# Splitting the downward weights of an FFN anew in every block instead of storing the parts

## The chip, the cores and the metric

The kernel runs on one core of a Trainium2 chip. The metric is the device time of one execution in microseconds, the median of several runs. TensorE (PE) multiplies, VectorE (DVE) and ScalarE (ACT) work elementwise, GpSimd (POOL) does small steps, and SyncE (SP) issues every DMA.

## The reference

One layer of a streaming encoder on 2048 new frames (a prompt) and on 32 frames of a running stream (a sample), width 1024, all in float32:

```
proj = rmsnorm(x) @ w_in                       # q, k, v, u, gate
o    = stick-breaking attention(q, k, v)       # 8 heads of 64
c    = silu(layernorm(dwconv31(u * sigmoid(gate))))
h    = x + concat([o, c]) @ w_out
up   = rmsnorm(h) @ w_up                       # 1024 -> 2 * 2816
a, g = split(dwconv3(up))
y    = h + (silu(g) * a) @ w_down              # 2816 -> 1024
```

The outputs are y of both streams, the new keys and values, and the states of the two convolutions. The change concerns the last line alone.

## The kernel before

**Split products.** Matmuls run on a float32r type. To keep float32 accuracy each operand is split into a high part (rounded to float32r) and a low part (the rest), and a product is the sum of three: high x high, low x high, high x low. The splitting is done by this helper:

```
def split(hi, lo, src):
    act(hi, src, AF.Copy)                                       # ScalarE
    vec.tensor_tensor(lo, src, hi.bitcast(F32), ALU.subtract)   # VectorE
```

**Stages.** A first phase makes q, k, v, u and gate for the whole prompt. Then the FFN runs in four blocks of 512 rows, `feed(0)` to `feed(3)`; the last block also takes the 32 rows of the sample. While blocks 0 to 2 run, other work is woven in: in block 0 the attention of the sample and part of the convolution, in block 1 the attention of rows 1024 and up, in block 2 its last part and the convolution of the last block; and in each of them `project` makes h of the next block. Block 3 has nothing woven in.

**Inside a block.** The 2816 channels are 22 tiles of 128 (f = 0 to 21; FT is 22). `up(f)` loads the up weights of two tiles (the linear and the gated half) in two parts each, multiplies, copies the sums out of PSUM (ScalarE), runs the 3-tap convolution (VectorE), applies silu and the product, and splits the result into `ah` and `al`. At its end it brings in wd, the downward weights of tile f: 128 rows of 1024, high and low. Tiles are taken in pairs (GRP is 2): `down` multiplies a pair after `up` of the first tile of the next pair, and VectorE adds the PSUM sums to y in SBUF. For the last pairs the order shifts by one: the pair 18, 19 is multiplied after `up(21)`, and the pair 20, 21 after that.

**Buffers.** SBUF is laid out by hand in two arenas, `arena` (float32) and `arena_r` (float32r). A name has a fixed list of places that are used in turn, by the order in which the program asks:

```
"raw": spots(8192, 512, 3),      # in arena: three pieces of 128x512
"jk": [9216],                    # the same words as the third raw
"wu": spots(24576, 2048, 2),     # in arena_r
"wd": spots(28672, 2048, 3),
"wdx": [26624],                  # the second wu
```

wd has three places, and the last tile of a block takes `wdx`. The raw pieces of w_up (block 0) and of w_out (`project`, by `out_weights`, which puts its parts into wu) go through the three places of `raw`. `norm_rows`, which norms h for the next block after `up(19)`, writes its squares to `jk`.

**Weights in DRAM.** In block 0 the raw weights are loaded, split, and both parts are stored to scratch tensors `wu_d` and `wd_d` in DRAM. Blocks 1 to 3 load the parts from there, 1 MB for each tile.

**Order.** The program is written as steps for a planner (`Plan`). It knows what every step reads and writes, gives each a price and a rank (the order in the program, or later if a step that it needs is later), simulates the five engines, and fixes an order of instructions for each engine, SP's DMA issues too. An engine takes the ready step of lowest rank. The DMA issues are one queue: an issue that waits (for a buffer to come free, say) holds up those behind it.

Of the kernel before, what the change touches and what calls it, by code (L numbers as in the profile page):

```python
# [11 lines left out]
F32R = mybir.dt.float32r  # L12
# [7 lines left out]
P = 128  # L20
# [12 lines left out]
FT = FF // P  # L33
# [338 lines left out]
def hybrid_step_kernel(  # L372
# [97 lines left out]
    def run(ap):  # L470

        n = 1
        for step, size in reversed(ap.ap):
            if step != n:
                break
            n *= size
        return n

    def dma(dst, src, gets=(), puts=()):
        dst, src = (x.bitcast(F32) if x.dtype == F32R else x for x in (dst, src))  # L480
        ns = dst.size() * 4 / 360 * (1 if min(run(dst), run(src)) >= 128 else 2)
        plan.add("sp", ns, lambda: nc.sync.dma_start(dst, src), [dst], [src], gets, puts)  # L482
# [9 lines left out]
    dram = ctx.enter_context(tc.tile_pool(name="dram", bufs=1, space=DRAM))  # L492
# [11 lines left out]
    c_d = dram.tile([SB, CB], F32, name="c_d")[:]  # L504

    wu_d = dram.tile([2 * FT, P, 2048], F32R, name="wu_d")[:]
    wd_d = dram.tile([FT, P, 2048], F32R, name="wd_d")[:]

    cst = ctx.enter_context(tc.tile_pool(name="cst", bufs=1))

# [42 lines left out]
    def slot(tag, shape, dtype=F32):  # L553
        at = SLOTS[tag]
        i = turns[tag] = (turns.get(tag, -1) + 1) % len(at)
        return place(at[i], shape, dtype)
# [22 lines left out]
    def split(hi, lo, src):  # L579
        act(hi, src, AF.Copy)  # L580
        vec.tensor_tensor(lo, src, hi.bitcast(F32), ALU.subtract)
# [631 lines left out]
    def feed(b, upto):  # L1213
# [5 lines left out]
        n = n_p + n_s  # L1219
# [18 lines left out]
        def up(f):  # L1238
            accs = []
            for part in range(2):  # L1240
                fi = part * FT + f
                wu = slot("wu", (2, KT, P), F32R)
                if b == 0:
                    for j in range(2):
                        raw = slot("raw", (4, P))
# [51 lines left out]
            ah, al = slot("ah" + tag, (w,), F32R), slot("al" + tag, (w,), F32R)  # L1297
            split(ah, al, aa)
            wd = slot("wdx" if f == FT - 1 else "wd", (2, D), F32R)
            if b == 0:  # L1300
                for j in range(2):
                    cs = slice(j * 512, (j + 1) * 512)
                    raw = slot("raw", (512,))
                    dma(raw, w_down[f * P : (f + 1) * P, cs])
                    split(wd[:, 0, cs], wd[:, 1, cs], raw)
                dma(wd_d[f], wd.rearrange("p a n -> p (a n)"), puts=[("wd", f)])
            else:
                dma(wd.rearrange("p a n -> p (a n)"), wd_d[f], gets=[("wd", f)])
            return ah, al, wd

        sums = slot("yc", (KT, PS + 2)) if n_s else None
# [185 lines left out]
```

## Time and profile before

| what | us |
|---|---|
| time, median of 3 runs | 2927.1 (2920.81 to 2928.97) |
| the profiled execution, its own time | 2924.49 |
| its span, from the first to the last instruction | 2922.7 |
| TensorE busy | 2729.2 |
| VectorE busy | 2041.6 |
| ScalarE busy | 1147.4 |

The profile is of one execution. Busy times of engines overlap, so they don't add up to the span. A time on its own in a row of a timeline or of the chain is counted from the start of the span.

### The profile page before, as it was taken

What the parts mean: (1) busy time and instruction counts of PE and PEld (TensorE: products, weight loads), DVE (VectorE), ACT (ScalarE), POOL (GpSimd) and SP (SyncE); (2) the same over time, 40 slices, a digit from 0 to 9 for tenths busy, and PEclk for the clock granted to TensorE, in tenths of its full rate; (3) what the DMA queues carried; (4) which work ended last, traced back from release to release, by engine and by line L of the source; (5) the groups of instructions that cost most, each with busy time, mean ns of one, the idle gap of its engine ahead of it and who ended that gap; (6) DMA issues with size and microseconds to landing.
All of it is one profiled execution on the core that took longest, in us unless ns stands there. A gap on an engine that the chain in (4) does not pass through costs nothing.

```text
span 2922.7 us, 42946 instructions
## 1 busy us (share of the span) xinstructions
PE 2729.2 (93%) x16218; PEld 2391.3 (82%) x16218; DVE 2041.6 (70%) x3055; ACT 1147.4 (39%) x2087; POOL 395.1 (14%) x809
## 2 busy tenths in 40 slices
PE   7998999989889999999999999999999979999999
PEld 7988898888767777778888877887777857899998
DVE  3476578679799776658887776779889745444444
ACT  4144434345544444435454454344444423211111
POOL 1144113224111010100000010001011000000000
PEclk9999999999899999999999999999999989999999
DMA  5255546654687998874555547664554466544443
GB/s 168 77 167 161 152 142 190 202 176 130 185 282 260 304 304 263 288 260 163 184 180 177 185 164 219 245 214 156 171 171 158 148 216 215 208 173 173 173 173 133
DMA packets 290696, 563.44 MB, mean 193 GB/s; under 512 B 33810, under 2 KB 175518, under 8 KB 256697
## 3 DMA queue, kind: packets, MB, share of 16 engines
q1 hardware_dynamic: 290489, 560.71, 58.4%
q8 instruction: 127, 2.08, 0.3%
q14 instruction: 80, 0.66, 0.1%
HBM read 410.14 MB, written 146.22 MB: 190 GB/s over the span
## 4 chain that ended last, share of the span: by engine, by line
PE 47%; DVE 13%; DMA 10%; ACT 4%; issue 4%; POOL 2%; SPq 1%; POOLq 0%; DVEq 0%; ACTq 0%
PE bank L424 44%; DVE arena L453 10%; DMA arena_r<-wu_d 4%; PE bank L431 3%; DVE arena_r L453 3%; ACT arena L438 2%; DMA arena<-in_w_up_dram 2%; ACT arena_r L438 1%; SPq L482 1%; ACT L438 1%; DMA h_d<-arena 1%; POOL arena L453 1%; POOL few L453 1%; DMA arena<-oT_d 1%; DMA arena<-in_w_out_dram 0%
## 5 line engine op out<-in xcount | busy, mean ns | idle before, releaser
L424 PE MATMUL bank<-arena_r 128*128 128x512 f32 (+6 forms) x14224 | 2544.8, 338 | 90.0 <-DMA arena_r<-wu_d 26.1
L424 PEld LDWEIGHTS bank<-arena_r 128*128 128x128 f32 x14224 | 2180.4, 192 | 378.8 <-DVE arena_r L453 33.1
L438 ACT ACTIVATE arena<-bank 128x512 f32<-128x512 f32 (+8 forms) x699 | 333.4, 501 | 859.4 <-PE bank L424 654.6
L438 ACT ACTIVATE arena_r<-arena 128x512 fp32r<-128x512 f32 (+2 forms) x428 | 288.4, 682 | 430.0 <-DVE arena L453 95.2
L453 DVE TENSOR_TENSOR arena<-bank,arena 128x512 f32<-128x512 f32 (+3 forms) x488 | 305.8, 635 | 182.5 <-PE bank L424 155.4
L453 DVE TENSOR_TENSOR_SCAN arena<-arena 128x512 f32<-128x512 f32 (+4 forms) x332 | 365.1, 1106 | 66.8 <-ACT arena L438 38.9
L453 DVE SCALAR_TENSOR_TENSOR arena<-arena,wdw 128x512 f32<-128x512 f32 (+1 forms) x600 | 402.0, 670 | 8.0
L453 DVE TENSOR_TENSOR arena_r<-arena,arena_r 128x512 fp32r<-128x512 f32 (+2 forms) x428 | 321.6, 765 | 105.8 <-ACT arena_r L438 103.5
L438 ACT ACTIVATE arena_r<-bank 128x512 fp32r<-128x512 f32 (+1 forms) x388 | 202.4, 562 | 283.0 <-PE bank L431 268.4
L431 PE MATMUL bank<-ident,arena 128*128 128x128 f32 (+5 forms) x1654 | 235.8, 279 | 74.1 <-DVE arena L453 59.6
L453 DVE TENSOR_SCALAR arena<-arena,wfd,bfd 128x512 f32<-128x512 f32 (+1 forms) x176 | 97.5, 554 | 293.6 <-ACT arena L438 293.6
L431 PEld LDWEIGHTS bank<-ident,arena 128*128 128x128 f32 (+5 forms) x1654 | 190.6, 143 | 114.9 <-DVE arena L453 77.8
L453 DVE SCALAR_TENSOR_TENSOR arena<-arena,wfd 128x512 f32<-128x512 f32 (+1 forms) x352 | 265.6, 755 | 8.7 <-DVE arena L453 0.5
L453 POOL COPY halo<-arena 128x2 f32<-128x2 f32 x220 | 55.6, 266 | 1293.0 <-ACT arena L438 1262.5
L453 DVE TENSOR_TENSOR arena_r<-bank,arena_r 128x512 fp32r<-128x512 f32 (+3 forms) x300 | 184.1, 640 | 56.7 <-ACT arena_r L438 55.9
L438 ACT ACT_TABLE_LOAD x107 | 137.3, 1283 | 8.5 <-DVE arena L453 5.5
L438 ACT ACTIVATE arena<-arena 128x512 f32<-128x512 f32 (+3 forms) x122 | 92.1, 756 | 110.3 <-DVE arena L453 97.3
L453 POOL TENSOR_SCALAR_AFFINE_SELECT arena<-arena 128x128 f32<-128x128 f32 x128 | 60.1, 476 | 426.5 <-ACT arena L438 423.7
L453 DVE TENSOR_TENSOR arena<-arena 128x512 f32<-128x512 f32 (+3 forms) x97 | 71.4, 736 | 61.8 <-ACT arena L438 35.0
L453 POOL TENSOR_TENSOR few<-few,nhalf 128x1 f32<-128x1 f32 (+3 forms) x87 | 101.3, 1164 | 7.1
L453 POOL TENSOR_SCALAR few<-few 128x1 f32<-128x1 f32 (+3 forms) x87 | 38.0, 437 | 446.4 <-DVE few L453 307.3
L453 POOL COPY arena<-halo 128x2 f32<-128x2 f32 x176 | 68.7, 391 | 184.6 <-DVE arena L453 177.9
(48 smaller groups left out, 449.9 us busy)
## 6 DMA issues: line engine op xcount, KB each, us to landing
arena_r<-wu_d SPq DMA_DIRECT2D x132, 1024.0 KB
arena_r<-wd_d SPq DMA_DIRECT2D x66, 1024.0 KB
wu_d<-arena_r SPq DMA_DIRECT2D x44, 1024.0 KB
arena<-in_w_up_dram SPq DMA_DIRECT2D x88, 256.0 KB
wd_d<-arena_r SPq DMA_DIRECT2D x22, 1024.0 KB
arena_r<-kT_d SPq DMA_DIRECT2D x80, 256.0 KB
arena_r<-dv_d SPq DMA_DIRECT2D x80, 256.0 KB
arena<-in_w_out_dram SPq DMA_DIRECT2D x80, 256.0 KB
```

The costliest lines, as they stand in the source:

```text
L424: lambda: nc.tensor.matmul(plan.real(out), lhsT, rhs, start=start, stop=stop),
L431: "pe", in_.shape[0] * (0.4167 if in_.dtype == F32R else 0.8333) + 2.5, lambda: nc.tensor.transpose(plan.real(out), in_, idt), [out], [in_ ...
L438: "act", ns, lambda: nc.scalar.activation(out, plan.real(in_), func, **kw), aps(out, kw.get("accum_out")), reads
L453: self.tag, self.price(name, n / (2 if fast else 1), pointers), lambda: fn(out, *map(plan.real, args), **kw), [out], aps(*args, *kw.values())
L482: plan.add("sp", ns, lambda: nc.sync.dma_start(dst, src), [dst], [src], gets, puts)
```

## The change

In every block, block 0 or not, each tile's downward weights are loaded raw in two pieces of 128x512 (256 KB) and split. The parts are no longer stored, and the scratch tensor `wd_d` is gone. The up weights are treated as before.

```diff
     wu_d = dram.tile([2 * FT, P, 2048], F32R, name="wu_d")[:]
-    wd_d = dram.tile([FT, P, 2048], F32R, name="wd_d")[:]
...
             wd = slot("wdx" if f == FT - 1 else "wd", (2, D), F32R)
-            if b == 0:
-                for j in range(2):
-                    cs = slice(j * 512, (j + 1) * 512)
-                    raw = slot("raw", (512,))
-                    dma(raw, w_down[f * P : (f + 1) * P, cs])
-                    split(wd[:, 0, cs], wd[:, 1, cs], raw)
-                dma(wd_d[f], wd.rearrange("p a n -> p (a n)"), puts=[("wd", f)])
-            else:
-                dma(wd.rearrange("p a n -> p (a n)"), wd_d[f], gets=[("wd", f)])
+            for j in range(2):
+                cs = slice(j * 512, (j + 1) * 512)
+                raw = slot("raw", (512,))
+                dma(raw, w_down[f * P : (f + 1) * P, cs])
+                split(wd[:, 0, cs], wd[:, 1, cs], raw)
             return ah, al, wd
```

## Rows read from the trace of the kernel before

**Rows 1.** The page: busy us, share of the span, instructions of each engine.

```profile
PE 2729.2 (93%) x16218; PEld 2391.3 (82%) x16218; DVE 2041.6 (70%) x3055; ACT 1147.4 (39%) x2087; POOL 395.1 (14%) x809
```

**Rows 2.** Busy times by stretch; its first row names the columns.

```profile
core 0: us, PE busy (x) PEld busy (x) DVE busy (x) ACT busy (x) POOL busy (x), PEclk, DMA share, GB/s
760.00:860.00 100.00, 81.27 (x376) 65.18 (x375) 84.11 (x132) 49.83 (x92) 16.86 (x32) 0.86 0.73 237
...
760.00:1260.00 500.00, 461.10 (x2113) 370.45 (x2113) 379.48 (x590) 236.28 (x392) 62.30 (x135) 0.96 0.84 275
1260.00:1835.00 575.00, 551.34 (x2862) 462.56 (x2861) 432.12 (x596) 259.58 (x437) 44.00 (x124) 0.99 0.57 190
1835.00:2330.00 495.00, 468.83 (x2400) 391.26 (x2399) 423.12 (x689) 214.40 (x354) 49.65 (x115) 0.99 0.52 180
2330.00:2412.00 82.00, 66.07 (x284) 50.09 (x283) 42.47 (x63) 22.32 (x39) 4.38 (x11) 0.90 0.68 214
2412.00:2923.00 511.00, 488.25 (x3309) 456.00 (x3307) 244.34 (x389) 100.09 (x247) 38.19 (x197) 0.99 0.50 179
2000.00:2240.00 240.00, 222.29 (x1146) 185.36 (x1145) 221.83 (x358) 98.71 (x166) 24.97 (x46) 0.99 0.48 163
```

**Rows 3.** Waits, 760 to 1260: engine, line, waited for, us, times, longest.

```profile
PE bank L424 <- ACT arena_r L438: 13.7, 6, 6.5
PE bank L424 <- DVE arena_r L453: 8.9, 10, 2.4
...
ACT arena_r L438 <- DMA arena<-in_w_up_dram: 60.9, 41, 4.5
```

**Rows 4.** Waits of TensorE, 1260 to 1835.

```profile
PE bank L431 <- DVE arena L453: 15.7, 14, 4.9
PE bank L424 <- DVE arena_r L453: 3.4, 3, 2.2
```

**Rows 5.** Waits of TensorE, 1835 to 2330.

```profile
PE bank L431 <- DVE arena L453: 12.8, 15, 1.6
PE bank L424 <- ACT arena L438: 6.2, 4, 2.2
PE bank L431 <- ACT arena L438: 3.8, 3, 1.5
```

**Rows 6.** Waits of TensorE, 2412 to the end.

```profile
PE bank L424 <- DMA arena_r<-wu_d: 14.4, 14, 2.4
```

**Rows 7.** The chain that ended last, by line: 1260 to 1835, then 1835 to 2330.

```profile
by line: PE bank L424 63.2%; DVE arena L453 7.9%; PE bank L431 7.3%; issue 6.4%; DMA arena_r<-wu_d 4.6%; ACT arena L438 3.1%; ACT L438 2.4%; DMA h_d<-arena 1.7%; DMA arena_r<-kT_d 1.4%; DVE arena_r L453 0.9%; DMA arena<-oT_d 0.8%; POOL aren
by line: PE bank L424 48.8%; DVE arena L453 26.4%; PE bank L431 6.1%; issue 4.0%; DVE arena_r L453 3.8%; ACT L438 3.4%; DMA arena_r<-wu_d 3.0%; ACT arena L438 2.8%; ACT arena_r L438 1.3%; POOL arena L453 0.3%; POOL halo L453 0.2%; ACTq L438
```

**Rows 8.** Groups by shape, 1260 to 1835: busy us, mean ns, idle before.

```profile
L453 DVE TENSOR_TENSOR arena_r<-arena,arena_r 128x512 fp32r<-128x512 f32 x39 | 26.3, 682 | 7.2 <-ACT arena_r L438 7.2
L438 ACT ACTIVATE arena_r<-arena 128x512 fp32r<-128x512 f32 x39 | 24.4, 629 | 17.3 <-DVE arena L453 10.6 <-PE bank L424 5.2 <-issue 1.2
```

**Rows 9.** Timeline of VectorE at 2442: start us, us, instruction.

```profile
2442.69 1.89 DVE L453 TENSOR_TENSOR arena_r<-arena,arena_r 128x512 fp32r<-128x512 f32 x3
```

**Rows 10.** Timeline of TensorE at the end of block 0: [idle before <- releaser].

```profile
1227.18 1.95 PE L424 MATMUL bank<-arena_r 128*128 128x512 f32 x3 [6.53 <-ACT arena_r L438]
```

**Rows 11.** Timeline of SP before block 3: issues of DMAs.

```profile
2383.49 0.84 SPq L482 DMA_DIRECT2D arena_r<-wd_d  x2
```

**Rows 12.** Pieces of the chain: start us, us from issue to landing.

```profile
769.63 3.62 DMA arena<-in_w_up_dram
...
2385.84 7.98 DMA arena<-in_w_out_dram
...
2599.80 6.62 DMA arena_r<-wu_d
...
2672.99 7.57 DMA arena_r<-wu_d
...
2877.88 6.40 DMA arena_r<-wu_d
```

## The prediction

> **What bounds the kernel now.** I read the page first. TensorE is busy for 2729.2 of 2922.7 us, VectorE for 2041.6 [rows 1]: what the change can win or lose is what TensorE waits, some 7% of the span, and not the sum of what it moves. The change touches only the four passes of the FFN, so I cut the span there: block 0 (760 to 1260 us), block 1 (to 1835), block 2 (to 2330), the hand-over to block 3 (to 2412), block 3 (to the end). The busy times of these stretches [rows 2] give TensorE's idle time: 39 us of 500, 24 of 575, 26 of 495, 16 of 82 and 23 of 511. Reading on in the same rows, the second engine differs by stage. In block 0 it is the DMA engines (share 0.84, 275 GB/s). In block 2 it is VectorE: 423.12 of 495 us, and 221.83 of 240 us from 2000 to 2240. In block 3 nothing else is near full (VectorE 244 of 511 us, DMA share 0.50).
>
> Then I asked what TensorE waits for in each stretch. In block 0 it is splits: 13.7 us on ScalarE's half, 8.9 us on VectorE's [rows 3], and ScalarE itself waits 60.9 us for raw up weights to land. In block 1 it waits for VectorE's scans (15.7 us) and differences (3.4 us) [rows 4]. In block 2 it waits for VectorE (12.8 us) and for ScalarE's copies and sigmoids (6.2 and 3.8 us) [rows 5]. In block 3 it is the landing of the up weights, 14.4 us in 14 waits [rows 6]. The chain of waits says the same: VectorE holds 26.4 + 3.8 = 30% of it in block 2 and 7.9 + 0.9 = 9% in block 1 [rows 7]. No row has TensorE waiting for the downward weights.
>
> **The change, part by part.** *Removed:* 22 stores of 1 MB, one for each f of block 0, and 66 loads of 1 MB in blocks 1 to 3. *Added:* in each of blocks 1 to 3, 44 raw loads of 256 KB, 44 copies on ScalarE and 44 subtractions on VectorE. Half the bytes are loaded, and the work goes to the two engines that TensorE already waits for.
>
> The same split of a 128x512 piece is in block 1 already: 629 ns for the copy, 682 ns for the difference [rows 8]. Instructions of VectorE overlap at their ends: three differences in a row took 1.89 us [rows 9], so one more costs (1.89 - 0.68) / 2 = 0.60 us of the engine. That is 44 x 0.60 = 26.4 us of VectorE and at most 44 x 0.63 = 27.7 us of ScalarE in a block of 500 to 575 us. ScalarE is busy for 260 of 575 us in block 1 and less elsewhere [rows 2], so its time is covered. Behind a copy that waits for its raw piece, or for the wd buffer that TensorE still reads, stand ScalarE's PSUM copies, for which VectorE and then TensorE wait. The planner puts the copy where it models the buffer as free, so I take nothing for that and leave it to the range.
>
> *Block 0.* Its bytes fall by 22 x 1.05 = 23 MB of 500 us x 275 GB/s = 137 MB, so the DMA share falls from 0.84 to about 0.70, and SP no longer holds a store back until VectorE has written the low half. What can come back is TensorE's wait for splits that wait for raw weights: of the 13.7 us [rows 3] one wait of 6.53 us is at the hand-over [rows 10], where ScalarE was busy with the norms of the next block; 7.2 us are left. Bounds 0 (the up weights keep their own chain of raw buffer, split and store) and -13.7. I take about half of the 7.2, -4 us, because most of the weights still moved are up weights.
>
> *Block 1.* Two readings. By the chain, VectorE sets 9% of the stretch: 0.088 x 26.4 = 2.3 us. By idle time: VectorE's goes from 575 - 432 = 143 us to 117, and if the 19.1 us that TensorE waits for it [rows 4] grow in that ratio (1.22), +4.2 us. I take +3; bounds 0 (the planner fits the splits into gaps) and +9, twice the second reading.
>
> *Block 2 to 2330.* Some 38 of the 44 splits lie here (495 of the 575 us or so between two hand-overs): 38 x 0.60 = 22.8 us on an engine with 72 us idle. By the chain: 0.302 x 22.8 = 6.9 us. By idle time: 72 / 49 = 1.47, and 22.8 us of waits for VectorE and ScalarE [rows 5] grow by 10.7 us. I take the chain's figure, +7, since the weight copies of this block may be put later, where VectorE is free; bounds 0 and +22.8, each split on the path.
>
> *Hand-over from block 2 to 3.* At 2383.49 two loads of 1 MB of wd are issued [rows 11], and the w_out piece behind them in the chain, issued at 2385.84, takes 7.98 us to land; a raw piece of the same 256 KB took 3.62 us at 769.63, the shortest that I found [rows 12]. ScalarE's copy of it, and TensorE behind that, can only come after. With a quarter of the bytes in each load ahead of it, at best 7.98 - 3.62 = 4.4 us come back; I take half, -2. On the other side the w_down pieces now pass through the same three raw buffers as the w_out pieces, and the third of them is also the scratch of the norms' squares (jk): up to +8.6 us, priced with the second rival.
>
> The Trainium skill speaks against this gain. Its page "DMA: Bandwidth & Descriptors" (Rules for kernel authors) asks for 1 MiB or more in one DMA, and its section "Anatomy of one DMA" fits a transfer as about 2.0 us plus the bytes at 436 GB/s, though for GpSimd's path: two pieces of 256 KB would be an estimated 5.2 us where one of 1 MB is 4.4, so halving the bytes would save no landing time. By that the hand-over gives 0 and not -2, block 3 too gains nothing, and the sum is +6. The rows agree that a small piece is dear (3.62 us for 256 KB against 6.40 us for 1 MB of wu), but not that two in flight cost twice that, which no row here shows.
>
> *Block 3.* Here TensorE waits for wu, and each load of it is issued when its buffer comes free. The waits are mostly at the first load after a pair's product, 4.4 us behind two wd loads of 1 MB: in the chain that load takes 6.62 to 7.57 us in five pairs (mean 7.03), and 6.40 us at 2877.88, with no wd near [rows 12]. Over 11 pairs 0.63 us each is 6.9 us. The raw pieces carry half the bytes, and they wait for a raw buffer and not for the wd buffer, so many will land earlier: I take -3, bounds -6.9 and 0. VectorE has half its time free here, so its 26.4 us cost nothing; without that cover they would be all of the cost. The last f's wd goes into a buffer (wdx) that up still reads; its raw pieces can land before that ends, and four short instructions then stand where a whole load stood.
>
> The sum is -4 + 3 + 7 - 2 - 3 = +1 us. The profiled execution took 2924.49 us (span 2922.7), so 2925.5 on its scale; the median of the three timed runs lies 2.6 us higher, at 2927.1, and on that scale I forecast **2928 us**. About 0.3% (8.8 us) is what a measurement can tell from no change; the three runs themselves spread over 8 us.
>
> **The rivals.** *First, VectorE becomes the bound of block 2 (slower).* Place: 2000 to 2240, where it is busy for 92% [rows 2]. Price: all 22.8 us there and the 4.2 us of block 1, less the 4 of block 0 and the 3 of block 3: +20, 2947 us. It decides when the convolution, scans and differences of that stretch can't move past 2240. For it: 30% of the chain. Against it: VectorE needs only 42 of 82 us from 2330 on, and the planner knows its price for each split.
>
> *Second, the raw buffers become the wait at the hand-overs (slower).* The downward pieces of f = 20 and 21 come behind the norms' squares in the third raw buffer, and these wait for the last rows of h. In block 0, where it is so already, TensorE lost 6.53 us at 1227 [rows 10]; I add a third for the splits that come late behind it: 8.6 us. At both later hand-overs that is +17 on top of +1: 2945 us (one alone 2937). It decides when the pieces land after TensorE has ended the product of f = 18 and 19. Against it: these products alone are 48 matmuls of 128x512, and the weights that they need are not held up.
>
> *Third, the freed DMA time is the larger part (faster).* Block 0 gives back all 13.7 us, the hand-over 4.4, block 3 6.9, and the splits find gaps in blocks 1 and 2 for all but 2 us: -23, 2904 us. For it: ScalarE's 60.9 us of waiting for raw up weights [rows 3], and the wu that lands late behind wd. Against it: TensorE is idle for 39 us in the whole block 0, and 18.7 us of that lies in its first 100 us [rows 2], where the FFN only starts.
>
> **How the numbers follow.** Chances: the forecast 0.43, first rival 0.20, second 0.14, third 0.23. The range is 2906 to 2948 us: it takes in the first two rivals and nearly reaches the third, whose time needs all its parts at their bounds. What it leaves out is mishaps added together above and such a full gain below. The forecast's own range is 2918 to 2938. Faster: 0.21 from the third rival and 0.03 from the forecast's lower edge, 0.24. Slower: 0.18 and 0.12 from the first two and 0.03 from the forecast's upper edge, 0.33. Within 0.3%: the rest, 0.43.
>
> **What would show it.** Block 0's DMA share near 0.70 and TensorE's waits for splits there some 4 us shorter; 83 copies and 83 differences of 128x512 (39 + 44) in block 1, and VectorE at 458 of 575 us; in block 2 a larger share of VectorE in the chain and 7 us more; in block 3 some 3 us less of waits for wu. The prediction is wrong if the planner, given other steps, orders a hand-over quite differently: one gap there is worth more than any of my terms. It is also wrong if ScalarE's copies wait for TensorE's buffers with the PSUM copies stuck behind them, which would show as waits of TensorE for ScalarE in block 3.

## The result, and the profile after

The changed kernel took 2908.03 us (median of 4 runs, 2898.65 to 2910.15) where the kernel before took 2926.45 on the same chip. The ratio is 0.9945, with a 95% interval of 0.9927 to 0.9962: 18 us less. A second comparison gave 2912.56 against 2919.88, ratio 0.9970 (0.9958 to 0.9982): 7 us less. Both are faster by more than the error. Their intervals just overlap; their mean is 13 us. The forecast, 1 us more than before (2928 us), lies 20 us above the time of the first comparison and some 14 us above the mean of the two.

The profiled execution of the changed kernel took 2898.65 us (span 2896.8). It is the fastest of the four by 9 us, so its profile shows the kernel at its best. Its busy times, to be set beside [rows 1]:

```profile
PE 2723.3 (94%) x16218; PEld 2387.5 (82%) x16218; DVE 2109.2 (73%) x3187; ACT 1221.9 (42%) x2217; POOL 402.4 (14%) x809
```

VectorE has 132 more instructions, as the change says (3 blocks of 44 splits), and 67.6 us more work. ScalarE has 74.5 us more: 132 more copies and two table loads fewer. TensorE's busy time is 6 us less and its idle time 20 us less (193.5 us before, 173.5 after). Its stretches, to be set beside [rows 2], with the same columns:

```profile
760.00:1260.00 500.00, 463.90 (x2118) 375.67 (x2118) 381.98 (x600) 238.77 (x393) 56.60 (x135) 0.96 0.74 232
1260.00:1835.00 575.00, 556.58 (x2908) 466.57 (x2908) 453.04 (x635) 286.64 (x487) 50.11 (x131) 1.00 0.55 177
1835.00:2330.00 495.00, 467.94 (x2386) 388.38 (x2385) 446.43 (x734) 235.12 (x391) 60.76 (x114) 0.99 0.47 154
2330.00:2412.00 82.00, 72.39 (x306) 55.54 (x305) 43.50 (x66) 21.33 (x37) 2.67 (x10) 0.94 0.67 207
2412.00:2897.00 485.00, 468.11 (x3230) 440.34 (x3228) 264.11 (x425) 124.20 (x288) 36.56 (x192) 0.99 0.46 157
2000.00:2240.00 240.00, 221.49 (x1120) 182.60 (x1119) 224.79 (x374) 110.16 (x182) 36.24 (x49) 0.98 0.46 149
```

VectorE's share rises in every stretch, and TensorE's falls in none by more than half a point. But these windows are fixed in time, so they hold different work in the two kernels once a gain has shifted it. The rest therefore goes by marks in the work: VectorE's first convolution step of each tile, read from its timeline. The time between two marks is the length of a stretch, whatever came before it. Single executions scatter by a few us in each stretch (the two profiles of the changed kernel have spans of 2896.8 and 2916.2 us), so the table takes the mean over all kernels profiled for this study that have the old path in a stretch, and over all that have the new one there (the kernel without the difference, below, is in none; a kernel that has the old path on one side of a hand-over and the new one on the other is left out of it; of block 3 only the plain old and new paths count, and the one with more places for wd). It is worked out from those timelines:

```
stretch (block, tiles)  old path there: n, mean (range)   new path there: n, mean (range)  difference
block 0, 0 to end       13  483.8 (481.4 to 487.2)         4  483.2 (480.1 to 487.4)   -0.6
block 1, 0 to 4          7   82.7 (80.9 to 86.1)          10   78.0 (77.4 to 78.8)     -4.7
block 1, 4 to 18        10  369.8 (368.0 to 371.4)         7  370.0 (368.0 to 371.3)   +0.2
hand-over 1 to 2        10  158.5 (156.3 to 160.9)         7  158.0 (153.1 to 160.1)   -0.6
block 2, 0 to 18        10  453.6 (452.0 to 455.5)         7  456.9 (455.1 to 457.7)   +3.3
hand-over 2 to 3         6  158.1 (155.9 to 159.6)         7  157.5 (155.7 to 160.5)   -0.6
block 3, 0 to 20         5  361.9 (360.1 to 363.5)         6  355.2 (354.6 to 356.1)   -6.7
```

A hand-over is from tile 18 of one block to tile 0 of the next. For block 0 the new path means that no stores of the downward parts stand in the plan. The differences add up to -9.7 us, between the two timed ones (-7 and -18). Two rows carry it, the first tiles of block 1 and block 3: in both the ranges of the two columns do not touch.

Two more numbers are used below. They are worked out from the same traces for the same stretches. One is TensorE's idle time. The other is what its clock costs: the trace records when the granted clock was 0.5, the lower of its two levels (1.2 GHz), and half of that time is counted as lost. In block 3 TensorE's idle time falls by 5.1 us and the clock's cost stays. In the first tiles of block 1 the idle time falls by 2.7 us and the clock's cost by 1.2. In block 2 the idle time grows by 1.2 us and the clock's cost by 1.4.

### The profile page after: what moved, and what is told of

Read it like the earlier page. It is cut to its first block, busy times and chain, and to the rows that moved or that the text cites. A ratio compares the mean times of both kernels' runs of the same rounds, so it can differ in the third digit from the quotient of the medians.

```text
span 2896.8 us, 43450 instructions
## 1 busy us (share of the span) xinstructions
PE 2723.3 (94%) x16218; PEld 2387.5 (82%) x16218; DVE 2109.2 (73%) x3187; ACT 1221.9 (42%) x2217; POOL 402.4 (14%) x809
## 4 chain that ended last, share of the span: by engine, by line
PE 45%; DVE 15%; DMA 9%; issue 5%; ACT 5%; SPq 1%; POOL 1%; POOLq 0%; ACTq 0%; DVEq 0%
PE bank L424 42%; DVE arena L453 11%; DVE arena_r L453 4%; PE bank L431 3%; ACT arena L438 2%; DMA arena_r<-wu_d 2%; DMA arena<-in_w_up_dram 2%; ACT arena_r L438 1%; ACT L438 1%; SPq L482 1%; DMA arena<-in_w_down_dram 1%; DMA arena<-in_w_out_dram 1%; POOL arena L453 1%; DMA arena_r<-qT_d 1%; DMA h_d<-arena 1%
## 5 line engine op out<-in xcount | busy, mean ns | idle before, releaser
L438 ACT ACTIVATE arena_r<-arena 128x512 fp32r<-128x512 f32 (+3 forms) x560 | 370.4, 671 | 552.6 <-PE bank L424 173.3
L453 DVE TENSOR_TENSOR arena_r<-arena,arena_r 128x512 fp32r<-128x512 f32 (+3 forms) x560 | 407.2, 739 | 149.9 <-ACT arena_r L438 147.0
L453 POOL COPY halo<-arena 128x2 f32<-128x2 f32 x220 | 62.0, 295 | 1246.0 <-ACT arena L438 1218.3
```

The source lines that it names most:

```text
L438: "act", ns, lambda: nc.scalar.activation(out, plan.real(in_), func, **kw), aps(out, kw.get("accum_out")), reads
L453: self.tag, self.price(name, n / (2 if fast else 1), pointers), lambda: fn(out, *map(plan.real, args), **kw), [out], aps(*args, *kw.values())
```

## The experiments

The theories: that the gain comes from the stores of block 0 (S in the expectations), from the halved bytes of the loads, or from their earlier issue; and that VectorE pays for it in blocks 1 and 2. Ratios are against the kernel before, run on the same chip, with 95% intervals.

**The stores of block 0.** My first reading of the two traces was that the gain came from block 0: TensorE's wait of 6.53 us at its end [rows 10] is gone in the changed kernel. Three kernels take it apart. The first keeps the stores in the changed kernel:

```diff
                 split(wd[:, 0, cs], wd[:, 1, cs], raw)
+            if b == 0:
+                dma(wd_d[f], wd.rearrange("p a n -> p (a n)"), puts=[("wd", f)])
```

> The changed kernel, with the 22 stores of both parts to a scratch tensor in block 0 kept, though nothing reads them; nothing else is undone. Theory S (the stores of block 0 were the cost: they fill the DMA queue and hold wd and raw buffers there): the early gain goes, about 10 us of it (in the profile after, the first step of the third tile of block 1 comes 11.7 us earlier than before, 1.2 of it from ahead of block 0), so some 2918 us. Theory R (the loads of blocks 1 to 3 are the cost: a load of both parts waits for the wd buffer that TensorE reads, and then lands beside the loads of up weights): within 3 us of the changed kernel, 2908. Theory P (the planner's new order at the hand-overs, by luck, is the gain): the order changes again, and the time may be anything between 2905 and 2930, the change showing at a hand-over and not inside a block.

Measured: 0.9973 (0.9961 to 0.9986). Still faster than before, with all the stores.

The second takes the stores out of the kernel before; blocks 1 to 3 load 1 MB from the scratch tensor of the up weights:

```diff
...
-                dma(wd_d[f], wd.rearrange("p a n -> p (a n)"), puts=[("wd", f)])
             else:
-                dma(wd.rearrange("p a n -> p (a n)"), wd_d[f], gets=[("wd", f)])
+                dma(wd.rearrange("p a n -> p (a n)"), wu_d[f], gets=[("wu", f)])
```

> The kernel before, without the stores of block 0; in blocks 1 to 3 wd is loaded in one piece of 1 MB as before, from the scratch tensor of the up weights, so y of these blocks is computed with other weights. Theory S: the gain of block 0 and its hand-over alone, about 10 us, so 2916; blocks 1 to 3 as before, with some 11 us of waits of TensorE for up weights in block 3. Theory R: no gain, 2926. Theory P: anything.

Measured: 0.9995 (0.9979 to 1.0011). Without the stores alone no gain is to be seen. The third has the first one's order, but each store moves 64 KB on the chip while the planner reckons with 1 MB (its edit against the first one, in short):

```diff
-                dma(wd_d[f], wd.rearrange("p a n -> p (a n)"), puts=[("wd", f)])
+                part = wd.rearrange("p a n -> p (a n)")[:, :128].bitcast(F32)
+                plan.add("sp", P * 2048 * 4 / 360, lambda: nc.sync.dma_start(wd_d[f][:, :128].bitcast(F32), part), ...)
```

> The changed kernel with the 22 stores of block 0 as steps of the planner, priced as 1 MB each, but of 64 KB on the chip: the order is that of the kernel with the stores kept, the traffic that of the changed one. Theory S by traffic (the stores held up the raw up weights in the DMA queue): the 6.5 us wait of TensorE for a split at the end of block 0 goes, and its time comes to that of the changed kernel, about 2908. Theory S by the order (the planner, with stores in its queue, puts the norms of the next block ahead of that split on ScalarE): the wait of 6.5 us stays, and the time is that of the kernel with the stores kept, 0.997 of before.

Measured: 0.9946 (0.9934 to 0.9958). TensorE's waits from 1180 to 1260 us, first of the changed kernel, then of this one:

```profile
PE bank L424 <- ACT arena_r L438: 3.3, 1, 3.3
```

```profile
PE bank L424 <- ACT arena_r L438: 6.9, 2, 6.5
```

The long wait comes back though the traffic stays away. So it belongs to the planned order, not to the bytes. It is also worth nothing on balance: without stores in the plan the tiles from 18 to 20 are 9 us shorter (37 us against 46 to 47), but tiles 8 to 16 are some 8 us longer (184 to 188 us against 175 to 179) and the way from 20 to block 1 another 3. The theory that the stores set the gain falls. This kernel was timed below the one that really stores (0.9946 against 0.9973, in two comparisons on two chips). The traces of the two hold the same instructions of VectorE, ScalarE, GpSimd and SyncE in the same order. Their profiles differ by 1.0 us in block 0, where the stores are, and by 9.0 us from there to tile 20 of block 3, where nothing is stored for wd. So a cost of the traffic does not show where it would have to arise, and what made the two comparisons differ is open.

**Block 3 alone.** The kernel before, with the new path in block 3 only:

```diff
-            if b == 0:
+            if b == 0 or last_b:
...
-                dma(wd_d[f], wd.rearrange("p a n -> p (a n)"), puts=[("wd", f)])
+                if b == 0:
+                    dma(wd_d[f], wd.rearrange("p a n -> p (a n)"), puts=[("wd", f)])
```

> The kernel before, but block 3 loads its downward weights raw and splits them; blocks 0 to 2 as before, with the stores. Theory R: block 3 is 6 to 9 us shorter (in the profiles, 25.9 less 16.9), all of it in waits of TensorE for up weights, 10.8 us to some 5; so about 2918. Theory S: no gain. Theory P: no gain in block 3, since nothing is woven in there and its order of matmuls is fixed.

Measured: 0.9994 (0.9982 to 1.0006), though its block 3 took 356.1 us like the changed kernel's. The hand-over ahead of it took 162.2 us, longer than in any kernel with the old path throughout (155.9 to 159.6): much of the gain was taken back there. More on that below.

Is it the earlier issue, or the fewer bytes? One kernel gives wd seven places in block 3, so that its loads need not wait for TensorE:

```diff
+    "wd3": spots(28672, 2048, 3, 0, 2048, 4096, 6144),
...
-            wd = slot("wdx" if f == FT - 1 else "wd", (2, D), F32R)
+            wd = slot("wd3" if last_b else "wdx" if f == FT - 1 else "wd", (2, D), F32R)
```

> The kernel before, but in block 3 wd has seven buffers and not three and one (four of them where the normed rows of blocks 0 to 2 lay), so that the loads of both parts can be issued several tiles ahead. The bytes and the engines' work are those of before. Theory R, by the wait for the buffer: the same 6 to 9 us in block 3 as from the raw loads, 2918. Theory B (it is the halved bytes in block 3): no gain, 2926, waits for up weights near 11 us.

Measured: 1.0009 (0.9996 to 1.0023), block 3 in 363.5 us. It is inconclusive on its own: the loads were free to go, but they still went out in pairs, 4.4 us ahead of the wu load. The next one adds the bytes back to the kernel with block 3 alone, as a second load of each raw piece to a place that nobody reads:

```diff
+    "dum": spots(9728, 512, 6),
...
+                    if last_b:
+                        dma(slot("dum", (512,)), w_down[f * P : (f + 1) * P, cs])
```

> Block 3 loads raw and splits (blocks 0 to 2 as before, stores kept), but every raw piece is followed by a second load of the same 256 KB to a place that nothing reads: 1 MB for each tile again, as before, in the place of the raw loads. If the halved bytes gave block 3 its gain, tile 0 to 20 goes back to some 362 us, with 9 us of waits for up weights; if it was that the raw loads are issued earlier and in pieces, it stays near 355, with 3 to 5 us of waits.

Measured: 1.0199 (1.0175 to 1.0222), and no answer. Since these loads depend on nothing, the planner put them first: SP's timeline shows one run of 32, and TensorE waited once for all of them at the hand-over (its waits from 2450 to 2600 us), not tile by tile.

```profile
2508.09 51.12 SPq L483 DMA_DIRECT2D arena<-in_w_down_dram  x32
```

```profile
PE bank L425 <- DMA arena_r<-wu_d: 55.5, 2, 52.0
```

The clean form of the question leaves everything where it was and halves the load, the high part alone:

```diff
-                dma(wd.rearrange("p a n -> p (a n)"), wd_d[f], gets=[("wd", f)])
+                if last_b:
+                    dma(wd[:, 0], wd_d[f][:, :D], gets=[("wd", f)])
+                else:
+                    dma(wd.rearrange("p a n -> p (a n)"), wd_d[f], gets=[("wd", f)])
```

> The kernel before, but in block 3 only the high part of wd is loaded, 512 KB for each tile, in the place of the old load (the low part there stays what block 2 left). If the halved bytes were the gain: tile 0 to 20 of block 3 near 355 us. If it was the earlier issue in pieces: near 362, waits for up weights near 9 us.

Measured: 0.9971 (0.9960 to 0.9982), block 3 in 352.5 us. TensorE's waits in block 3, in the kernel before (2510 to 2923 us) and in this one (2512 to 2914 us):

```profile
PE bank L424 <- DMA arena_r<-wu_d: 10.8, 11, 2.2
```

```profile
PE bank L424 <- DMA arena_r<-wu_d: 2.1, 1, 2.1
```

The traces of these two kernels hold the same instructions of VectorE, ScalarE, GpSimd and SyncE in the same order; only the size of these loads differs. So halved bytes are enough: no split, no raw buffer, no earlier issue.

The traces also show what the bytes do. The semaphore updates tell when each load landed, waited for or not. In block 3 there are ten loads of wu that come next behind wd loads or pieces. The first, at the hand-over, took 8.75 to 10.84 us in these three kernels and is left out of this table of times from issue to landing, in us:

```
block 3                              before               half loads           changed
wu right behind wd, mean of 9         6.57 (5.71 to 7.57)  4.83 (4.71 to 4.97)  4.87 (4.68 to 5.41)
every other wu load, median of 33     4.84                 4.84                 4.90
last wd still under way after the
issue of that wu, mean                3.1                  0.9                  0.9
```

Behind two loads of 1 MB, wu takes 1.7 us longer than elsewhere in the block. Behind half the bytes it takes no longer than elsewhere: the wd loads have all but landed when it is issued.

**Without the difference.** The changed kernel, but in blocks 1 to 3 only the high part is made:

```diff
-                split(wd[:, 0, cs], wd[:, 1, cs], raw)
+                if b == 0:
+                    split(wd[:, 0, cs], wd[:, 1, cs], raw)
+                else:
+                    act(wd[:, 0, cs], raw, AF.Copy)
```

> The changed kernel without VectorE's difference in blocks 1 to 3 (the low part of wd there stays what block 0 left). It prices VectorE's added work. By my step for block 2 (VectorE sets 30% of the chain there): tile 0 to tile 18 of block 2 falls from 457 us to some 452, block 1 by 1 to 3 us, block 3 not. By the first rival (all of it on the path): block 2 falls by over 15 us. If VectorE's work is hidden: no difference anywhere.

Measured: 0.9946 (0.9932 to 0.9961). Block 2 took 453.2 us, what it takes with the old path (453.6 in the mean) and 3.7 less than the new path: so the cost in block 2 comes with VectorE's differences. It is not all waiting: of the 3.3 us in the table, 1.2 are idle time of TensorE and 1.4 the lower clock. The plan of this kernel changes too (its hand-over 1 to 2 took 162 us), so only that stretch is read.

**The two kernels once more**, beside those above:

> The changed kernel once more, for a second profile and a closer ratio. If the gains of the first profile at the hand-overs 1 to 2 and 2 to 3 (5.6 and 3.9 us, from the last steps of one block to the first of the next) belong to the order of its instructions, they come again; if they were the luck of one execution, they don't, and the span is some 2906 us. Block 3 again near 405 us, the stretch of block 2 from its first to its 18th tile near 457 us, and the ratio near 0.995.

> The kernel before once more, for a second profile: block 3 near 413.6 us, block 2 from tile 0 to 18 near 452.4, the hand-over 0 to 1 (tile 18 to tile 2) near 132 us, 1 to 2 (tile 18 to tile 0) near 158.7, 2 to 3 near 159.6. What differs by more than 1 us from the first profile is not to be read from single profiles.

Measured: the ratio of 0.9970 given above for the changed kernel, and 2928.32 us in one execution of the other. Its block 3 took 361.8 us against 355.2 in the changed kernel's second profile; the gain there repeats, while the short hand-over 1 to 2 of the changed kernel's first profile (153.1 us) does not (157.5).

**The first tiles of block 1.** The table's second row was first only read off kernels that differ in more than that. This one has the new path in four tiles of block 1 and nowhere else:

```diff
-            if b == 0:
+            if b == 0 or (b == 1 and f < 4):
...
-                dma(wd_d[f], wd.rearrange("p a n -> p (a n)"), puts=[("wd", f)])
+                if b == 0:
+                    dma(wd_d[f], wd.rearrange("p a n -> p (a n)"), puts=[("wd", f)])
```

> The kernel before, with the raw pieces and splits in the first four tiles of block 1 alone; stores and full loads otherwise. Theory B (a wu load at the start of block 1 is late because three 1 MB loads of wd stand ahead of it): the stretch from tile 0 to tile 2 of block 1 falls from 38 to 42 us to 32 to 34 us, the rest stays, 6 us in all, ratio 0.998. Rival (the gain there comes from another order of block 0, or from the missing traffic of its stores): 38 to 42 us, ratio 1.000.

Measured: 0.9988 (0.9976 to 1.0000), 3.5 us, at the edge of what the comparison can tell. Tiles 0 to 2 took 33.4 us, and tiles 0 to 4 78.4 us, as in the changed kernel (77.6 and 78.2) and not as before (82.3 and 86.1). SP's timeline there, first of the kernel before, then of this one:

```profile
1267.83 1.01 SPq L482 DMA_DIRECT2D arena_r<-wd_d  x2
...
1279.39 0.33 SPq L482 DMA_DIRECT2D arena_r<-wu_d  x1
1279.77 0.42 SPq L482 DMA_DIRECT2D arena_r<-wd_d  x1
...
1284.83 0.32 SPq L482 DMA_DIRECT2D arena_r<-wu_d  x1
```

```profile
1265.91 1.52 SPq L482 DMA_DIRECT2D arena<-in_w_down_dram  x2
...
1275.17 0.33 SPq L482 DMA_DIRECT2D arena_r<-wu_d  x1
1275.59 1.39 SPq L482 DMA_DIRECT2D arena<-in_w_down_dram  x1
...
1280.61 0.32 SPq L482 DMA_DIRECT2D arena_r<-wu_d  x1
```

The chain of waits holds one of these loads of wu in each; its piece before, and then here (start, us from issue to landing):

```profile
1284.83 11.63 DMA arena_r<-wu_d
```

```profile
1275.17 7.66 DMA arena_r<-wu_d
```

Before, three loads of 1 MB of wd and one of wu stood ahead of the load at 1284.83, which took 11.63 us. By the semaphore updates the first two of wd had landed by then; one of wd, one of wu, two of h and a store were still under way. With raw pieces the chain has one of 7.66 us, the first of the two loads; the second took 8.58 us and is not waited for. Both go out 4.2 us earlier, and so does VectorE's mark of tile 0 (1281.31 us, before 1285.53): in the work's own time they are issued as before, and the second lands sooner. From mark to mark (tiles 0 to 4) the rows are these, in the kernel before and in this one; the first two numbers are the stretch and TensorE's busy time, the third last its granted clock:

```profile
1285.53:1367.81 82.28, 78.82 (x392) 65.04 (x391) 56.62 (x81) 37.84 (x61) 7.71 (x23) 0.98 0.57 200
```

```profile
1281.31:1359.67 78.36, 76.53 (x392) 63.88 (x391) 58.90 (x85) 39.83 (x65) 8.24 (x23) 1.00 0.60 202
```

The same number of matmuls takes 3.9 us less: 1.6 us less idle time and 2.3 us less busy time. Part of the second is the clock. Before, TensorE is idle for 1.6 of the 4 us from 1322, waiting for VectorE, and then the granted clock falls to the lower level for most of this row:

```profile
1326.00:1330.00 4.00, 3.95 (x14) 3.41 (x15) 3.65 (x6) 2.17 (x4) 0.69 (x3) 0.57 0.17 72
```

Of the seven profiles with the old path there, four have such a fall in these tiles; of the ten with the new path, none. That the bytes do it here too, as in block 3, is not shown by itself: this edit also changes the order of the plan, and no half load was tried in block 1.

**Both places, and the best version.** The same with block 3 as well:

```diff
-            if b == 0:
+            if b == 0 or last_b or (b == 1 and f < 4):
...
-                dma(wd_d[f], wd.rearrange("p a n -> p (a n)"), puts=[("wd", f)])
+                if b == 0:
+                    dma(wd_d[f], wd.rearrange("p a n -> p (a n)"), puts=[("wd", f)])
```

> The kernel before, with raw pieces and splits in the first four tiles of block 1 and in all of block 3. Theory B: the two gains are local and add up, 6 us at the start of block 1 and 8 us in block 3, with none of the cost of the splits in block 2 (4 us): about 14 us, ratio 0.995. Rival (each is taken back at the next hand-over, as the run with block 3 alone gave only 0.9994): ratio 0.998 to 1.000.

Measured: 0.9967 (0.9956 to 0.9979), 9.6 us. Block 3 took 355.6 us, tiles 0 to 4 of block 1 78.3, but the hand-over 2 to 3 163.3 us. So the theory is right in both places, and its rival right in part: some 4 us are taken back at the last hand-over. All three kernels with the old path in block 2 and the new one in block 3 show it (162.2, 163.3 and 161.7 us; they are in neither column of the table there). It is not the bytes, since the kernel with half loads in block 3 took 158.7 us there. Of the 4.2 us in the mean, 2.5 are idle time of TensorE (its waits for wu are 1.8 us longer than in the six kernels of the table's old column, those for ScalarE's splits 1.1) and 1.7 the lower clock. Why they grow is open.

What remains of TensorE's waits in block 3 is wu's own two places. The changed kernel with four:

```diff
+    "wu3": [24576, 26624, 0, 2048],
...
-                wu = slot("wu", (2, KT, P), F32R)
+                wu = slot("wu3" if last_b else "wu", (2, KT, P), F32R)
```

> The changed kernel with four buffers for the up weights in block 3 in place of two (the added two lie where the normed rows of blocks 0 to 2 lay). If TensorE's waits for up weights in block 3 are nothing but the buffer coming free too late, the 4 to 5 us left of them go: block 3 from tile 0 to 20 near 350 us, and 0.2% less than the changed kernel, some 0.994 of before.

Measured: 0.9932 (0.9916 to 0.9948), block 3 in 348.7 us. The same edit on the kernel with 64 KB stores, twice:

> The same four buffers, with the planner's order of the kernel whose stores are steps of 1 MB for the planner and of 64 KB on the chip. That one took 0.9946 of before; with block 3 near 350 us, 0.993, some 2900 us: the version that would beat both.

Measured: 0.9925 (0.9909 to 0.9942), block 3 in 347.8 us.

> The kernel that was best so far (changed kernel, order planned with 1 MB stores, 64 KB stored, four places for wu in block 3), on the same chip as the other three: 0.9925, as the last time; the bound of what one comparison can tell is how far it moves from that.

Measured: 0.9935 (0.9917 to 0.9954). And on the kernel with the new path at both ends alone:

> The same, with four places for wu in block 3. Theory B: 7 us less again in block 3 (tiles 0 to 20 in 348 us), ratio 0.993. It also asks which version is best: if the splits of the middle of block 1 and of block 2 cost what their stages show (5 us), this one is as far below the changed kernel with four places for wu, 0.991. Rival (the missing loads of 1 MB in block 2 pay for the splits there): not below 0.993.

Measured: 0.9944 (0.9924 to 0.9964), block 3 in 347.5 us. The rival has it: leaving block 2 on the old path saves 3.3 us there and loses some 4 at the hand-over. The changed kernel with four places for wu in block 3 is the lowest of those without the 64 KB stores, at 0.9932, but its interval overlaps that of the last one. The 64 KB stores on top of it (0.9925 and 0.9935) add nothing that can be told. TensorE's waits for wu from 2412 us to the end, 14.4 us before [rows 6], are these in it:

```profile
PE bank L425 <- DMA arena_r<-wu_d: 2.8, 3, 1.3
```

## Why the prediction was wrong

The forecast was a sum of +1 us; the stretches give about -10. Three steps were too high: block 3 by 3.7 us, the first tiles of block 1 by 4.7, and the splits of VectorE in blocks 1 and 2 by 6.5 together. Block 0 and the hand-over from 2 to 3 were too low, by 4.7 together.

**Block 3: the right mechanism at less than half its size.** The mechanism that I named, wu landing late behind wd, is the one that the kernel with half loads shows. Of the bound of -6.9 I took -3, because half the bytes are still loaded. It measured -6.7. The answer to [rows 6], to the end of the span:

```profile
PE bank L424 <- DMA arena_r<-wu_d: 5.6, 6, 2.6
```

14 waits have become 6, and 14.4 us 5.6. The chain of block 3, first of the kernel before (2510 to 2923 us), where ten loads of wu stand in it, then of the changed one (2493 to 2897 us), where four do; the longest and the shortest of these are shown:

```profile
by line: PE bank L424 82.6%; DMA arena_r<-wu_d 16.4%; PE bank L431 0.7%; issue 0.5%; DMA out_dram<-arena 0.3%; ACT arena L438 0.1%; ACTq L438 0.0%
```

```profile
by line: PE bank L424 92.8%; DMA arena_r<-wu_d 6.6%; PE bank L431 0.7%; DMA out_dram<-arena 0.3%; issue 0.2%; ACT arena L438 0.1%; ACTq L438 0.0%
...
2486.71 7.16 DMA arena_r<-wu_d
...
2852.39 6.08 DMA arena_r<-wu_d
```

The loads still in the chain are hardly shorter than those of [rows 12], and that misled me: a load stands in the chain only when it came late. The loads that nobody waited for are not there, and they are most of them. So two readings of the prediction were wrong. The load with no wd near (6.40 us) was itself a late one; by the table under the half loads a wu load by itself takes 4.84 us. And the pairs in which the load behind wd took less than 6.62 us (down to 5.71) were left out of the mean of 7.03; over nine pairs it is 6.57. The delay behind wd was 1.7 us and not 0.63. The failed step is "I take -3": scaling the delay by the bytes. With half the bytes it does not halve, it is gone (4.87 us), because wd has all but landed before wu is issued. That the bound of -6.9 came out so nearly is luck, as it was worked out from the 0.63. What came back is waits: in block 3 TensorE waited 10.8 us for wu before, in 11 waits, and 4.7 us after, in 4. The busy share of the DMA engines over 20 us, in forty slices, shows it, before (from 2595 us: the wd pair, then wu, without a break) and after (from 2574 us: the raw pieces, then wu by itself):

```profile
DMA  0092698998989999978310091899970001000945
```

```profile
DMA  0002947421878509179896100006469999100019
```

The kernel with half loads shows that the bytes do it by themselves, and also that my other reason (the pieces "wait for a raw buffer and not for the wd buffer") is not needed. The pieces do go out earlier, 6.1 us ahead of wu instead of 4.4; SP's timeline before, and after:

```profile
2595.39 0.80 SPq L482 DMA_DIRECT2D arena_r<-wd_d  x2
2599.80 0.32 SPq L482 DMA_DIRECT2D arena_r<-wu_d  x1
```

```profile
2574.77 4.27 SPq L482 DMA_DIRECT2D arena<-in_w_down_dram  x4
2580.89 18.36 SPq L482 DMA_DIRECT2D arena_r<-wu_d  x4
```

The estimate that the prediction weighed against this gain does not carry over to this queue: with it block 3 gains nothing, and the measured gain is 6.7 us. It was worked out from the Trainium skill's page "DMA: Bandwidth & Descriptors" ("Anatomy of one DMA"), whose fit is for one DMA on GpSimd's path. What went wrong is adding up two such times: the four raw pieces of a pair are under way together and land within 2.5 to 4.0 us of their issue (2574 to 2582 us in the changed kernel).

**Block 1: a gain was not priced at all.** I entered block 1 as cost alone (+3). Its first four tiles gained 4.7 us, most likely by the mechanism that I had named for block 3: a wu load behind 1 MB loads of wd. The failed step is that this term was put at nothing. I had looked at the hand-over into block 3 and not at the one into block 1, where the load of 11.63 us stood in the same trace. By "No row has TensorE waiting for the downward weights" I had passed over the loads that wait behind them.

**The splits cost VectorE less than either reading.** In block 1 I took +3 and in block 2 +7; tiles 4 to 18 of block 1 gave +0.2, block 2 +3.3. The work itself was sized nearly right: 67.6 us of VectorE in all, where 3 x 26.4 = 79 were foreseen. From 1260 to 1835 us the groups have 77 copies and 77 differences where 83 were foreseen, at the same durations as in [rows 8]:

```profile
L453 DVE TENSOR_TENSOR arena_r<-arena,arena_r 128x512 fp32r<-128x512 f32 x77 | 51.8, 683 | 12.0 <-ACT arena_r L438 12.0
L438 ACT ACTIVATE arena_r<-arena 128x512 fp32r<-128x512 f32 x77 | 48.2, 634 | 49.3 <-PE bank L424 21.2 <-DVE arena L453 12.3 <-DMA arena<-in_w_down_dram 11.1
```

VectorE is busy for 453 us there (458 foreseen). The chain of block 2 went as foreseen, from 30.2% on VectorE [rows 7] to 38.2%:

```profile
by line: PE bank L424 43.0%; DVE arena L453 31.7%; DVE arena_r L453 6.5%; PE bank L431 5.2%; ACT L438 3.6%; ACT arena L438 3.1%; issue 3.0%; DMA arena_r<-wu_d 1.9%; ACT arena_r L438 1.5%; POOL arena L453 0.1%; POOL halo L453 0.1%; ACTq L438
```

The failed step is the factor: an instruction of 0.60 us was charged at the share of the chain that VectorE held, as if it fell at random. The 20.9 us by which VectorE is busier from 1260 to 1835 found room at no cost that can be measured (tiles 4 to 18 of block 1). In block 2 half of the chain's figure was paid. That the planner's placing of the splits is the reason is argued and not shown: no run places them otherwise.

**Block 0: the waits fell, the block did not get shorter.** I took -4 and measured -0.6. The DMA share fell as foreseen (0.74; 0.70 foreseen), and so did TensorE's waits for splits, from 13.7 and 8.9 us [rows 3] to these (760 to 1260 us):

```profile
PE bank L431 <- DVE arena L453: 15.7, 9, 2.8
PE bank L424 <- ACT arena_r L438: 8.7, 3, 4.4
PE bank L431 <- DVE arena_r L453: 3.3, 3, 2.4
PE bank L424 <- DVE arena_r L453: 3.2, 3, 2.4
```

The waits of line 424 for splits are 10.7 us less, more than I took. But TensorE waits longer for VectorE's other work in exchange (15.7 us, before 11.0, the row below), and the block is no shorter. As the kernels with and without stores show, the freed DMA time gave nothing here: without the stores a different order is planned, and what it wins at the end of the block it loses in the middle.

```profile
PE bank L431 <- DVE arena L453: 11.0, 10, 2.8
```

**The hand-over from block 2 to 3: the step as foreseen, and given back.** The w_out piece that took 7.98 us [rows 12] takes 3.23 without the 1 MB loads ahead of it, near the 3.62 of my bound; in the kernel with both ends changed, which keeps those loads in block 2, it takes 8.27. The chain's piece after, then in that kernel:

```profile
2373.48 3.23 DMA arena<-in_w_out_dram
```

```profile
2384.73 8.27 DMA arena<-in_w_out_dram
```

TensorE's wait for the split of that piece (6.1 us before, 6.3 there) is down to 0.5. Its waits in the whole hand-over, before and after:

```profile
PE bank L424 <- DMA arena_r<-wu_d: 12.0, 4, 8.3
PE bank L424 <- ACT arena_r L438: 7.4, 2, 6.1
PE bank L424 <- DVE arena_r L453: 2.2, 2, 1.4
```

```profile
PE bank L424 <- DMA arena_r<-wu_d: 7.5, 3, 6.6
PE bank L424 <- DVE arena_r L453: 5.1, 7, 1.5
PE bank L424 <- ACT arena_r L438: 3.9, 3, 2.0
```

VectorE's differences are now waited for seven times instead of twice. In the mean over the kernels the tiles 18 to 20 gain 3.2 us and the rest of the hand-over loses 2.6: -0.6 in all, where I had -2.

**The rivals.** The first did not come: block 2 lost 3.3 us and not 22.8; from 2000 to 2240 us VectorE's busy time rose from 221.8 to 224.8 of 240 only. The splits did not keep out of that window: it holds 25 of VectorE's differences of this form, and 8 before. Other steps of VectorE left it (78 of one step of the convolution, 87 before, and 43 scans, 45 before), some of them only because the window is fixed in time. The second did not come either. It feared 8.6 us at each of the later hand-overs. From 1 to 2 TensorE's waits for splits were 2.2 us before and 3.5 and 4.7 in the two profiles of the changed kernel; from 2 to 3 those for VectorE's differences rose by 2.9 us and those for ScalarE's copies fell by 3.5. ScalarE waits more for raw downward pieces, 88.1 us in 49 waits over the whole kernel (33.8 in 18 before); TensorE's waits for ScalarE's splits did not grow with it in block 0, at the hand-over from 2 to 3 or in block 3:

```profile
  ACT arena_r L438: 88.1, 49
```

The third rival was the nearest: block 3 at its bound and the splits almost free. It failed in block 0, where its largest part (13.7 us) was to come from, and the first tiles of block 1 stood in for some of it.

**What stays open:** why one comparison gave 18 us and the other 7. The two profiles of the changed kernel are 19 us apart, with the same instructions of VectorE, ScalarE, GpSimd and SyncE in the same order, and most of that goes with the clock: the mean granted clock was 0.980 in the first and 0.974 in the second, and 0.006 of 2900 us is an estimated 17 us. In block 0, where they differ by 7.2 us, the same 2065 matmuls ran at 0.98 and at 0.96:

```profile
799.84:1279.98 480.14, 452.51 (x2065) 366.22 (x2064) 366.23 (x578) 215.24 (x347) 50.30 (x123) 0.98 0.74 234
```

```profile
803.00:1290.37 487.37, 458.09 (x2065) 370.36 (x2064) 366.73 (x578) 215.58 (x347) 51.31 (x123) 0.96 0.73 231
```

Why the clock is lower in one execution than in another is not shown, and the two comparisons are medians of several executions, for which this does not settle the matter. Open too: the 4 us at the hand-over 2 to 3 when block 3 is changed and block 2 is not; and why the kernel with real stores and the one with 64 KB stores were timed at 0.9973 and 0.9946.

## What to carry to other kernels

When a change takes bytes out of a queue, look for the loads that stand behind them, in every place where the pattern occurs, rather than for waits on the bytes themselves: here nothing waited for the removed loads, and the gain in block 3 was in the loads behind them. Take the time of a load by itself from loads that nobody waited for; the chain of waits shows only the late ones (6.1 to 7.6 us here, where most took 4.8). A delay behind other loads can vanish whole when they get smaller, so price it by the waits that it causes and not by the share of the bytes. Work added to VectorE cost nothing that can be measured where it was 75% busy (block 1), and half of its share of the chain where it was 85% busy (block 2). A kernel with a changed plan is compared by marks in the work and over several kernels, and with the granted clock beside each stretch, since one gap or one fall of the clock in one profile may be worth more than the change.

## What was not expected of the hardware

A piece of w_out of 256 KB landed in 3.23 us with other 256 KB pieces about, and in 8.27 us behind loads of 1 MB. Most 1 MB loads of wu took 4.8 us in block 3; right behind two loads of 1 MB they took 5.7 to 7.6, and behind two of 512 KB 4.8 again. One took 11.63 us at the start of block 1, with five other transfers under way. Four pieces of 256 KB in a row delay the next load no more than two of 512 KB do. The same program, with the same order of instructions, ran at a mean granted clock of 0.974 and of 0.980, and took 19 us longer at the first. The kernel before, run 34 times on one chip, took 2913.22 to 2931.13 us: one execution tells nothing below 0.6%, and even two comparisons of the same pair gave 0.9945 and 0.9970.
